# GpSimd products for a third of the key chunks, and TensorE transposes of q and k, in a hybrid attention block

## The chip, the cores and the metric

The kernel runs on one core of a Trainium2 chip. The metric is device time in microseconds (us) of one execution. The core has five engines that run their own instruction streams in order and meet at semaphores: TensorE (PE; its weight loads are listed apart as PEld), VectorE (DVE), ScalarE (ACT), GpSimd (POOL) and SyncE (SP), which here only issues DMAs. Lines such as L563 are lines of the kernel before; in the changed kernel everything behind the edits stands 12 to 14 lines further down.

## The reference

One layer of a residual trunk, 2048 tokens of width 1024 in float32: RMSNorm, one combined projection, four heads of differential attention and eight heads of stick-breaking attention, an output projection, RMSNorm and a SwiGLU feed-forward block (2816 wide). The change lies in the stick-breaking part:

```python
def one_block(args):
    qb, blk = args
    q_pos = blk * QBLK + jnp.arange(QBLK, dtype=jnp.int32)
    z = jnp.einsum('bqhd,bkhd->bhqk', qb, k).astype(jnp.float32) * scale
    mask = (k_pos[None, :] < q_pos[:, None])[None, None]
    log_1mb = jnp.where(mask, jax.nn.log_sigmoid(-z), 0.0)
    rem = lax.cumsum(log_1mb, axis=3, reverse=True) - log_1mb
    a = jnp.where(mask, jnp.exp(jax.nn.log_sigmoid(z) + rem), 0.0)
    return jnp.einsum('bhqk,bkhd->bqhd', a.astype(v.dtype), v)
```

With beta = sigmoid(z), the weight of key s for query t is beta(t,s) times the product of 1 - beta over the keys between s and t.

## The kernel before

Matrix products are made in fp16 with both operands split into a high and a low half, three products for one. The heads are worked in eight groups g: 0 to 3 hold one differential head each, 4 to 7 two stick-breaking heads each. While group g is in attention, a stream (`proj_stream`) projects group g+1: 16 token tiles of 24 matmuls (L325) into one of two PSUM banks tagged "pj", read out as v and as q and k by `proj_out` (casts L332 or L334, residuals L335). After every fourth tile `proj_batch` transposes q and k: two DMA transposes of 8 blocks of 128x128 from the tile st into qT[:, 2:4] and kT (L377), and two DMA copies that exchange the upper and lower 64 partitions of q into qT[:, 0:2] (L379). So the score matmuls have a q with high and low half swapped. All of these DMAs stand in SP's one queue.

A stick-breaking group runs 48 units (`stage_a`): a query tile i of 128 rows, a head m and a block b of up to 1024 keys. A unit takes two tiles of a ring of nine ("z4", 128x1028 float32), om and be. Per chunk of up to 512 keys, from the last to the first: scores in a PSUM bank sc (L453, four banks); ACT writes sigmoid(-z) into om (L559) and sigmoid(z) = beta back into the score bank (L560); DVE scans om backwards to running products (L562; the score bank is its second operand, which the operation bypasses); DVE multiplies beta and the shifted om into be (L563). Then `split_t` casts be to fp16 on ACT (L89, tile s of a ring of three), subtracts for the low half on GpSimd (L98), and a DMA transposes both halves into aT (L408). Five units later `stage_b` multiplies aT with v on PE (L463).

A helper chooses engines when the program is built: `pick` adds an operation's cost to a ledger for each engine and takes the one with the lowest sum, and `level` clears the ledgers at every fourth query tile. `note` books work that has no choice. Casts (`to16`: L89 ACT, L91 DVE, L93 GpSimd), `tt` and `split_psum` are chosen so. The order of each engine's instructions is then made by a scheduler that simulates the program; it is fixed before the run.

The output projection of finished token tiles (L766) starts beside the last group, and the FFN follows from about 1465 us on.

Of the kernel before, what the change touches and what calls it, by code (L numbers as in the profile page):

```python
# [11 lines left out]
F32 = mybir.dt.float32  # L12
F16 = mybir.dt.float16
BF16 = mybir.dt.bfloat16
I32 = mybir.dt.int32
AF = mybir.ActivationFunctionType
ALU = mybir.AluOpType
# [4 lines left out]
S, D, P = 2048, 1024, 128  # L22
# [37 lines left out]
def block(tc, a, out):  # L60
    nc = tc.nc
    PE, ACT, DVE, POOL, SP = nc.tensor, nc.scalar, nc.vector, nc.gpsimd, nc.sync
    top = ExitStack()
    with top:
# [8 lines left out]
        def note(e, ns):  # L73
            load[e] += ns * KW[e]

        def pick(**cost):
            e = min(cost, key=lambda k: load[k] + cost[k] * KW[k])
            load[e] += cost[e] * KW[e]
            return e

        def level():
            for k in load:
                load[k] = 0.0

        def to16(dst, src, n, engines="ADP", psum=False):
            cost = {"A": 0.84 * n + 110, "D": (1.05 if psum else 0.53) * n + 70, "P": 1.1 * n + 80}
            e = pick(**{k: cost[k] for k in engines})
            if e == "A":
                ACT.copy(dst, src)  # L89
            elif e == "D":  # L90
                DVE.tensor_copy(dst, src)  # L91
            else:
                POOL.tensor_scalar(dst, src, 1.0, 0.0, op0=ALU.mult, op1=ALU.add)  # L93

        def tt(dst, a_, b_, op, n, engines="DP"):
            cost = {"D": 1.15 * n + 70, "P": 2.45 * n + 80}
            e = pick(**{k: cost[k] for k in engines})
            (DVE if e == "D" else POOL).tensor_tensor(dst, a_, b_, op)  # L98

        def pri(k):  # L100
            def deco(f):
                @functools.wraps(f)
                def g(*args):
                    with tc.high_priority(PRI[k]) if PRI[k] else nullcontext():
                        return f(*args)
                return g
            return deco

        def nm(s):
            uid[0] += 1  # L110
            return f"{s}{uid[0]}"
# [7 lines left out]
        id16 = cp.tile([P, P], F16, name="id16")  # L119
# [25 lines left out]
        def rstd(dst, ss, mul, eps):  # L145
            n = dst.shape[-1]
            if n > 1:
                ACT.activation(dst, ss, AF.Identity, bias=eps, scale=mul)
            else:
                DVE.tensor_scalar(dst, ss, mul, eps, op0=ALU.mult, op1=ALU.add)  # L150
            POOL.tensor_tensor(dst, dst, mhalf[:, :n], ALU.pow)
# [100 lines left out]
        psj = top.enter_context(tc.tile_pool(name="psj", bufs=2, space=PSUM, side="right"))  # L252
# [3 lines left out]
        with ExitStack() as ph1:  # L256
# [6 lines left out]
            def z4():  # L263
                return zp.tile([P, 1028], F32, tag="z4", bufs=ZB, name=nm("z4"))
# [87 lines left out]
            @pri("pb")  # L352
            def proj_batch(g, G, B):
                st, v, raw = B
                qT = sp.tile([P, 4, 4, P], F16, tag="qT", bufs=QB, name=nm("qT"))
                kT = sp.tile([P, 2, 4, P], F16, tag="kT", bufs=KB, name=nm("kT"))
                if g < 4:
                    rq = raw[:].rearrange("p t (c e) -> p t c e", e=64)
                    sq = st[:].rearrange("p c t s e -> p (c t s e)")[:, :2048].bitcast(F32)
                    ACT.activation(sq.rearrange("p (t c e) -> p t c e", t=4, c=4), rq, AF.Square)  # L360
                    note("A", 950)
                    ss = sm.tile([P, 16], F32, tag="ss", bufs=2, name=nm("ss"))
                    DVE.tensor_reduce(ss[:], sq.rearrange("p (c e) -> p c e", e=64), op=ALU.add, axis=AX.X)
                    rs = sm.tile([P, 16], F32, tag="rs", bufs=2, name=nm("rs"))
                    rstd(rs[:], ss[:], 2.0 ** -16 / 64, G["epsk"][:])
                    rsb = rs[:].rearrange("p (t c) -> p t c", c=4).unsqueeze(3).to_broadcast([P, 4, 4, 64])
                    DVE.tensor_tensor(rq, rq, rsb, ALU.mult)
                    note("D", 2300)
                    gb = gk[:].unsqueeze(1).unsqueeze(1).to_broadcast([P, 4, 2, 64])
                    tt(rq[:, :, 2:4, :], rq[:, :, 2:4, :], gb, ALU.mult, 512)  # L370
                    for o in range(2):
                        src = rq[:, :, 2 * o : 2 * o + 2, :]
                        d = st[:, 2 * o : 2 * o + 2].rearrange("p c t s e -> p t c s e")
                        to16(d[:, :, :, 0, :], src, 512)
                        tt(d[:, :, :, 1, :], src, d[:, :, :, 0, :], ALU.subtract, 512)
                for T, c in ((qT[:, 2:4], 0), (kT[:], 2)):
                    SP.dma_start_transpose(T.rearrange("p c t n -> p (c t) n"), st[:, c : c + 2].rearrange("p c t s e -> p (c t s e)"))  # L377
                for o in (0, 64):
                    SP.dma_start(qT[o : o + 64, 0:2].rearrange("p c t n -> p (c t n)"), qT[64 - o : 128 - o, 2:4].rearrange("p c t n -> p (c t n)"))  # L379
                G["q"].append(qT)  # L380
                G["k"].append(kT)
                G["v"].append(v)
# [63 lines left out]
            def fq(g, i):  # L446
                k = 2 if g == NG - 1 else 4
                return (i % k, k)
# [92 lines left out]
            def sb_attn(g, G):  # L541
                last = {}

                @pri("at")
                def stage_a(i, m, b):
                    L = (i + 1) * 128
                    n = min(1024, L - 1024 * b)
                    be, om = z4(), z4()
                    if b == i // 8:
                        DVE.memset(om[:, n : n + 1], 8192.0)  # L550
                    else:
                        DVE.tensor_copy(om[:, n : n + 1], last[m][:, 0:1])
                    last[m] = om
                    for c in range((n - 1) // 512, -1, -1):
                        lo, hi = 512 * c, min(512 * c + 512, n)
                        w = hi - lo
                        sc = ps.tile([P, 512], F32, tag="sc", bufs=4, name=nm("sc"))
                        score_chunk(G, sc, i, 2 * b + c, m, w // P, b == i // 8 and hi == n)
                        ACT.activation(om[:, lo:hi], sc[:, :w], AF.Sigmoid, scale=G["nkz"][:])  # L559
                        ACT.activation(sc[:, :w], sc[:, :w], AF.Sigmoid, scale=G["kz"][:])  # L560
                        ov = om[:, lo:hi][:, ::-1]
                        DVE.tensor_tensor_scan(ov, ov, sc[:, :w], om[:, hi : hi + 1], op0=ALU.mult, op1=ALU.bypass)  # L562
                        DVE.tensor_tensor(be[:, lo:hi], sc[:, :w], om[:, lo + 1 : hi + 1], ALU.mult)  # L563
                        note("A", 1.7 * w + 400)
                        note("D", 3.15 * w + 350)
                    return n, split_t(be[:, :n], n, "A", "P")

                ypd = {}

                def stage_b(i, m, b, n, aT):  # L570
                    r, k = fq(g, i)
                    if i // k not in ypd:
                        ypd[i // k] = ps.tile([P, 512], F32, tag="yp", name=nm("yp"))
                    yp = ypd[i // k]
                    pv(G, yp, P * r + 64 * m, aT, b, n, 128 * m, 64, r == 0 and m == 0 and b == i // 8, r == k - 1 and m == 1 and b == 0)
                    if m == 1 and b == 0 and r == k - 1:
                        finish(g, G, i, k, yp)
                        G["fin"] = i + 1

                pend = []  # L580
                done = 0
                for i in range(NT):
                    if i % 4 == 0:
                        level()
                    for b in range(i // 8, -1, -1):
                        for m in range(2):
                            n, aT = stage_a(i, m, b)
                            pend.append((i, m, b, n, aT))
                            if len(pend) > PD:
                                stage_b(*pend.pop(0))  # L590
                            done += n // P + CS
                            yield done / (272 + 48 * CS), (i + 1 if b == 0 and m == 1 else i)
                for u in pend:
                    stage_b(*u)
# [640 lines left out]
```

## Time and profile before

| | us |
|---|---|
| median of 3 runs (2754.74 to 2759.51) | 2757.65 |
| profiled execution | 2755.86 |
| its span, first to last instruction | 2754.1 |
| first and last stick-breaking scan (L562) starts | 612.6 and 1395.6 |
| last projection weight load (L325) starts | 1203.4 |
| first FFN weight load (L943) starts | 1465.0 |

The profile gives each engine's busy time and the span in 40 slices of 68.9 us with busy tenths. A row of a group of instructions has line, engine, operation, output and inputs, shapes and count; then busy us and the mean ns of one; then the engine's idle time just before them and what ended it. A row of waits has who waited for whom, us in total, times, longest us. Granted clock is the TensorE clock that the throttle granted, 1 being full speed.

### The profile page before, as it was taken

Reading aid. Unit: us, or ns where it says so; the run is one execution under the profiler, and the core shown is the slowest. Engines: PE = TensorE matmul, PEld = TensorE weight load, DVE = VectorE, ACT = ScalarE, POOL = GpSimd, SP = SyncE. Lnnn points to the kernel's source line nnn. Section 1 sums busy time; section 2 is a strip of 40 time slices with the busy share of each in tenths; the row PEclk is TensorE's granted clock in tenths of the full one; section 3 lists DMA queues with packets and bytes.
Section 4 is the critical chain, followed back from the end, with each engine's and each line's share of the span. In section 5 each row is a group of like instructions: output and inputs, shape, how many; then the busy total and the mean of one; then the engine's idle time right before and its main releaser. Section 6 shows DMA issues by size and latency. Waiting matters only on the chain. (4 is left out here: it accounts for less than half of the span.)

```text
span 2754.1 us, 45485 instructions
## 1 busy us (share of the span) xinstructions
PE 2491.4 (90%) x17084; PEld 1411.9 (51%) x17084; DVE 1997.4 (73%) x3782; ACT 1361.3 (49%) x2543; POOL 1447.6 (53%) x1008
## 2 busy tenths in 40 slices
PE   7998989888888786888989899999999999999998
PEld 4665555555555453457775444444444444444443
DVE  6898879787889989986655877777785544444445
ACT  4665656566878778765644535444352212111121
POOL 2578767655455545546565656565574232322323
PEclk9999999999999987999999999999999999999999
DMA  6788787789999988987797675656658834635534
GB/s 225 201 170 184 148 189 163 173 172 203 196 217 191 198 175 156 199 196 208 199 272 273 218 241 199 220 196 226 235 182 307 315 146 164 229 136 198 207 121 167
DMA packets 649133, 551.91 MB, mean 200 GB/s; under 512 B 506624, under 2 KB 574208, under 8 KB 638672
## 3 DMA queue, kind: packets, MB, share of 16 engines
q1 hardware_dynamic: 647088, 546.92, 72.0%
q8 instruction: 134, 2.20, 0.3%
q0 software_dynamic: 512, 1.36, 0.2%
q10 hardware_dynamic: 1312, 0.72, 0.1%
q14 instruction: 87, 0.71, 0.1%
HBM read 265.27 MB, written 151.52 MB: 151 GB/s over the span
## 5 line engine op out<-in xcount | busy, mean ns | idle before, releaser
L98 POOL TENSOR_TENSOR s<-z,s 128x1024 f16<-128x1024 f32 (+7 forms) x288 | 473.9, 1653 | 334.1 <-ACT s L89 291.2
L325 PE MATMUL pj<-w,xt 128*128 128x384 f16 x3072 | 572.2, 334 | 29.3 <-DVE st L335 12.1
L325 PEld LDWEIGHTS <-xt 128*128 128x128 f16 x3072 | 300.2, 100 | 239.9 <-issue 37.3
L453 PE MATMUL sc<-kT,qT 128*128 128x512 f16 (+3 forms) x1280 | 348.7, 363 | 72.0 <-DVE z L563 33.0
L1041 PE MATMUL pd<-wd,act 128*128 128x512 f16 x1848 | 406.0, 379 | 3.4 <-DVE hs L1047 2.4
L562 DVE TENSOR_TENSOR_SCAN z<-z,sc 128x512 f32<-128x512 f32 (+3 forms) x320 | 355.5, 1113 | 69.4 <-ACT sc L560 67.5
L463 PE MATMUL yp<-v,aT 128*128 128x64 f16 (+1 forms) x4896 | 282.0, 208 | 76.4 <-DMA aT<-s 75.7
L463 PEld LDWEIGHTS <-aT 128*128 128x128 f16 x4896 | 246.5, 102 | 165.1 <-DMA aT<-s 101.7
L943 PEld LDWEIGHTS <-wg 128*128 128x128 f16 x1848 | 182.3, 99 | 247.3 <-issue 37.3
L1041 PEld LDWEIGHTS <-act 128*128 128x128 f16 x1848 | 180.7, 98 | 222.3 <-issue 4.6
L943 PEld LDWEIGHTS <-wu 128*128 128x128 f16 x1848 | 181.8, 98 | 219.7 <-issue 7.2
L98 POOL TENSOR_TENSOR hs<-hs,cu 128x512 f32<-128x512 f32 x132 | 166.8, 1268 | 239.8 <-DVE cu L1047 86.3
L98 POOL TENSOR_TENSOR act<-cg,act 128x512 f16<-128x512 f32 x117 | 166.6, 1437 | 231.4 <-ACT act L999 125.1
L98 POOL TENSOR_TENSOR fst<-fst 128x512 f32<-128x512 f32 x97 | 182.5, 1882 | 157.3 <-DVE wd L220 85.9
L1047 DVE SCALAR_TENSOR_TENSOR hs<-pd,c,hs 128x512 f32<-128x512 f32 x192 | 142.3, 749 | 163.0 <-PE pd L1041 161.5
L89 ACT CAST s<-z 128x384 f16<-128x384 f32 (+7 forms) x216 | 170.2, 789 | 151.5 <-DMA aT<-s 61.9
L559 ACT ACTIVATE z<-sc,c 128x512 f32<-128x512 f32 (+3 forms) x320 | 203.3, 635 | 10.2 <-PE sc L453 6.7
L563 DVE TENSOR_TENSOR z<-sc,z 128x512 f32<-128x512 f32 (+3 forms) x320 | 193.4, 606 | 8.1
L560 ACT ACTIVATE sc<-sc,c 128x512 f32<-128x512 f32 (+3 forms) x320 | 195.6, 611 | 0.0
L999 ACT CAST act<-cg 128x512 f16<-128x512 f32 x132 | 81.3, 616 | 222.1 <-DVE cg L1005 175.8
L766 PE MATMUL po<-wo,mt 128*128 128x256 f16 x1536 | 182.0, 277 | 6.9 <-DVE xf L769 4.9
L943 PE MATMUL pm<-X,wg 128*128 128x512 f16 x792 | 179.1, 379 | 0.2 <-ACT bx L1116 0.2
(233 smaller groups left out, 4026.5 us busy)
## 6 DMA issues: line engine op xcount, KB each, us to landing
xt<-xs SPq DMA_DIRECT2D x112, 512.0 KB, 4.4
hs<-hd SPq DMA_DIRECT2D x96, 512.0 KB, 4.3
hd<-hs SPq DMA_DIRECT2D x80, 512.0 KB, 3.5
split<-wg SPq DMA_DIRECT2D x11, 1792.0 KB, 11.4
split<-wu SPq DMA_DIRECT2D x11, 1792.0 KB, 10.3
split<-wd SPq DMA_DIRECT2D x11, 1792.0 KB, 10.5
wg<-split SPq DMA_DIRECT2D x11, 1792.0 KB, 7.2
wd<-split SPq DMA_DIRECT2D x11, 1792.0 KB, 8.2
```

Of the source, the lines that this page charges most:

```text
L89: ACT.copy(dst, src)
L98: (DVE if e == "D" else POOL).tensor_tensor(dst, a_, b_, op)
L325: PE.matmul(pj[:, :384], lhsT=xv[:, xi, kt, :], rhs=G["w"][:, wi, kt, :], start=n == 0, stop=n == 23)
L453: PE.matmul(sc[:, : 128 * w].rearrange("p (t n) -> p t n", n=P), lhsT=G["q"][i // 4][:, 2 - 2 * o + m, i % 4, :], rhs=G["k"][q][:, m, 0:w, ...
L463: PE.matmul(yp[:, y0 : y0 + wd], lhsT=aT[:, a_, :], rhs=v[:, v_ : v_ + wd], start=start and j == 0 and q == 0, stop=stop and j == nb - 1 a ...
L559: ACT.activation(om[:, lo:hi], sc[:, :w], AF.Sigmoid, scale=G["nkz"][:])
L560: ACT.activation(sc[:, :w], sc[:, :w], AF.Sigmoid, scale=G["kz"][:])
L562: DVE.tensor_tensor_scan(ov, ov, sc[:, :w], om[:, hi : hi + 1], op0=ALU.mult, op1=ALU.bypass)
L563: DVE.tensor_tensor(be[:, lo:hi], sc[:, :w], om[:, lo + 1 : hi + 1], ALU.mult)
L766: PE.matmul(po[:, sl], lhsT=mt[:, kt, P * xi : P * xi + P], rhs=wos[2 * h + n][wi][:, kt, :], start=q == 0, stop=q == 23)
L943: PE.matmul(ps_[:].rearrange("p (t n) -> p t n", n=P), lhsT=wv[:, wo, wi, 128 * kt : 128 * kt + 128], rhs=X[xo][:, :, xi, kt, :], start=st ...
L1041: PE.matmul(po[:], lhsT=act[:, ao, xi, 128 * j : 128 * j + 128], rhs=W["d"][:, wo, wi, :], start=start and u == 0 and q == 0, stop=u == nu ...
```

## The change

In `stage_a` each chunk's product may go to GpSimd. `pick` compares DVE at 1.04 w + 155 ns and GpSimd at 2.4 w + 100 ns for w keys. If GpSimd is taken, ACT writes beta to be in SBUF and not to the score bank, and GpSimd multiplies be by om in place; the scan then has the raw scores as its bypassed operand.

In `proj_batch`, for groups 5 to 7, PE transposes q and k into a "pj" bank, seen as 1024 fp16 columns: one bank for kT, one for qT[:, 2:4], one for the swapped qT[:, 0:2], whose blocks are made in two halves of 64 rows. ACT or DVE copies each bank out. The DMA transposes and copies stay for groups 0 to 4.

```diff
-                for T, c in ((qT[:, 2:4], 0), (kT[:], 2)):
-                    SP.dma_start_transpose(T.rearrange("p c t n -> p (c t) n"), st[:, c : c + 2].rearrange("p c t s e -> p (c t s e)"))
-                for o in (0, 64):
-                    SP.dma_start(qT[o : o + 64, 0:2].rearrange("p c t n -> p (c t n)"), qT[64 - o : 128 - o, 2:4].rearrange("p c t n -> p (c t n)"))
+                if g > 4:
+                    for T, c, sw in ((kT[:], 2, 0), (qT[:, 2:4], 0, 0), (qT[:, 0:2], 0, 1)):
+                        pt = psj.tile([P, 512], F32, tag="pj", name=nm("qkt"))[:].bitcast(F16)
+                        for b in range(8):
+                            blk = st[:, c + b // 4, b % 4]
+                            if sw:
+                                for o in range(2):
+                                    PE.transpose(pt[64 * o : 64 * o + 64, P * b : P * b + P], blk[:, 1 - o, :], id16[:])
+                            else:
+                                PE.transpose(pt[:, P * b : P * b + P], blk.rearrange("p s e -> p (s e)"), id16[:])
+                        to16(T.rearrange("p c t n -> p (c t n)"), pt, 1024, "AD", True)
+                else:
+                    ...
                         ACT.activation(om[:, lo:hi], sc[:, :w], AF.Sigmoid, scale=G["nkz"][:])
-                        ACT.activation(sc[:, :w], sc[:, :w], AF.Sigmoid, scale=G["kz"][:])
+                        e = pick(D=1.04 * w + 155, P=2.4 * w + 100)
+                        beta = sc[:, :w] if e == "D" else be[:, lo:hi]
+                        ACT.activation(beta, sc[:, :w], AF.Sigmoid, scale=G["kz"][:])
                         ov = om[:, lo:hi][:, ::-1]
                         DVE.tensor_tensor_scan(ov, ov, sc[:, :w], om[:, hi : hi + 1], op0=ALU.mult, op1=ALU.bypass)
-                        DVE.tensor_tensor(be[:, lo:hi], sc[:, :w], om[:, lo + 1 : hi + 1], ALU.mult)
+                        (DVE if e == "D" else POOL).tensor_tensor(be[:, lo:hi], beta, om[:, lo + 1 : hi + 1], ALU.mult)
                         note("A", 1.7 * w + 400)
-                        note("D", 3.15 * w + 350)
+                        note("D", 2.08 * w + 200)
```

The order of the built programs shows where the instructions stand. On GpSimd, in group 4 (be is z_9302, z_9342, z_9367 and so on, one a unit; s is the fp16 pair), before:

```order
L98 TENSOR_TENSOR s_9313<-z_9302,s_9313 128x512
L98 TENSOR_TENSOR s_9353<-z_9342,s_9353 128x512
L98 TENSOR_TENSOR s_9384<-z_9367,s_9384 128x1024
L98 TENSOR_TENSOR s_9415<-z_9398,s_9415 128x1024
L98 TENSOR_TENSOR s_9495<-z_9477,s_9495 128x640
```

and in the changed kernel, at the same units:

```order
L98 TENSOR_TENSOR s_9313<-z_9302,s_9313 128x512
L577 TENSOR_TENSOR z_9367<-z_9367,z_9368 128x512 x2
L98 TENSOR_TENSOR s_9353<-z_9342,s_9353 128x512
L577 TENSOR_TENSOR z_9477<-z_9477,z_9478 128x512
L98 TENSOR_TENSOR s_9384<-z_9367,s_9384 128x1024
L98 TENSOR_TENSOR s_9415<-z_9398,s_9415 128x1024
L98 TENSOR_TENSOR s_9495<-z_9477,s_9495 128x640
```

Products (L577) of newer units now stand between the residuals of older ones. On DVE, at the unit of z_9367 and z_9368, before (a scan is printed as a SCALAR_TENSOR_TENSOR of L562):

```order
L562 SCALAR_TENSOR_TENSOR z_9368<-z_9368,sc_9370 128x512
L563 TENSOR_TENSOR z_9367<-sc_9370,z_9368 128x512
L552 COPY z_9399<-z_9343 128x1
L562 SCALAR_TENSOR_TENSOR z_9368<-z_9368,sc_9377 128x512
L335 SCALAR_TENSOR_TENSOR st_10013<-pj_10132,st_10013 128x4x64
L563 TENSOR_TENSOR z_9367<-sc_9377,z_9368 128x512
L562 SCALAR_TENSOR_TENSOR z_9399<-z_9399,sc_9401 128x512
```

and now:

```order
L576 SCALAR_TENSOR_TENSOR z_9368<-z_9368,sc_9370 128x512
L91 COPY kT_9872<-qkt_9873 128x1024
L576 SCALAR_TENSOR_TENSOR z_9368<-z_9368,sc_9377 128x512
L576 SCALAR_TENSOR_TENSOR z_9399<-z_9399,sc_9401 128x512
L91 COPY qT_9871<-qkt_9893 128x1024
L577 TENSOR_TENSOR z_9398<-sc_9401,z_9399 128x512
```

Both products of this unit are gone from DVE, and two copies of transposed q and k stand between the scans. On SP, in the same group, before (qT and kT are the transposed q and k, aT the transposed weights, xt an input tile of the projection):

```order
L408 DMA_TRANSPOSE aT_9545<-s_9542 128x10x128
L377 DMA_TRANSPOSE qT_10403<-st_10013 128x8x128
L377 DMA_TRANSPOSE kT_10404<-st_10013 128x8x128
L408 DMA_TRANSPOSE aT_9610<-s_9607 128x16x128
L379 DMA qT_10403<-qT_10403 64x1024
L408 DMA_TRANSPOSE aT_9644<-s_9641 128x16x128
L379 DMA qT_10403<-qT_10403 64x1024
```

and now:

```order
L420 DMA_TRANSPOSE aT_9545<-s_9542 128x10x128
L420 DMA_TRANSPOSE aT_9610<-s_9607 128x16x128
L403 DMA xt_10884<-xs 128x2048
L420 DMA_TRANSPOSE aT_9644<-s_9641 128x16x128
```

The four DMAs of the batch have left SP's queue. On PE, before, this stretch has no matmul on st; now, inside a projection tile (qkt is the bank of the transposes, id the identity):

```order
L325 MATMUL pj_10408<-w_8277,xt_10406 128x384
L385 LDWEIGHTS st_10047
L385 MATMUL qkt_10439<-id_68,st_10047 128x128
L385 LDWEIGHTS st_10047
L385 MATMUL qkt_10439<-id_68,st_10047 128x128
L385 LDWEIGHTS st_10047
L385 MATMUL qkt_10439<-id_68,st_10047 128x128
L325 LDWEIGHTS xt_10406
```

Three transposes of a batch stand between matmuls of one projection tile; the others follow in runs of up to 16, with attention work between the runs.

More of the change, by code (lines that the diff above doesn't have):

```diff
@@ L375, in proj_batch @@
                         tt(d[:, :, :, 1, :], src, d[:, :, :, 0, :], ALU.subtract, 512)
-                for T, c in ((qT[:, 2:4], 0), (kT[:], 2)):
-                    SP.dma_start_transpose(T.rearrange("p c t n -> p (c t) n"), st[:, c : c + 2].rearrange("p c t s e -> p (c t s e)"))
-                for o in (0, 64):
-                    SP.dma_start(qT[o : o + 64, 0:2].rearrange("p c t n -> p (c t n)"), qT[64 - o : 128 - o, 2:4].rearrange("p c t n -> p (c t n)"))
+                if g > 4:
[10 more added lines that the diff above has]
+                else:
+                    for T, c in ((qT[:, 2:4], 0), (kT[:], 2)):
+                        SP.dma_start_transpose(T.rearrange("p c t n -> p (c t) n"), st[:, c : c + 2].rearrange("p c t s e -> p (c t s e)"))
+                    for o in (0, 64):
+                        SP.dma_start(qT[o : o + 64, 0:2].rearrange("p c t n -> p (c t n)"), qT[64 - o : 128 - o, 2:4].rearrange("p c t n -> p (c t n)"))
                 G["q"].append(qT)
```

## The prediction

> **What bounds the kernel now.** First the page's shares, for the whole program.
>
> ```profile
> PE 2491.4 (90%) x17084; PEld 1411.9 (51%) x17084; DVE 1997.4 (73%) x3782; ACT 1361.3 (49%) x2543; POOL 1447.6 (53%) x1008
> PE   7998989888888786888989899999999999999998
> DVE  6898879787889989986655877777785544444445
> ```
>
> PE looks like the bound, but the share is a mean over stages: in slices 9 to 17 (about 610 to 1200 us) DVE shows 9 where PE shows 8 or less. That is stick-breaking attention, the only place that the change touches. So next the busy time by stretch (columns: us, then PE, PEld, DVE, ACT, POOL busy with counts, granted clock, DMA share, GB/s).
>
> ```profile
> 612.00:1200.00 588.00, 473.07 (x4803) 295.59 (x4801) 519.51 (x933) 457.75 (x880) 304.46 (x196) 0.92 0.95 192
> 1200.00:1400.00 200.00, 176.13 (x1826) 145.15 (x1825) 144.86 (x235) 123.42 (x212) 115.22 (x79) 0.96 0.78 198
> 1700.00:2754.00 1054.00, 1021.83 (x4741) 465.82 (x4739) 607.13 (x831) 281.01 (x379) 447.68 (x315) 0.99 0.56 203
> ```
>
> From 612 to 1200 DVE is busy 519.5 of 588 us (88%), PE 80%, ACT 78%, GpSimd 52%, and the DMA engines 95%. From 1200 to 1400 the output projection fills PE (88%) and DVE has room; the FFN is PE's (97%). So what the change can win lies in the 588 us, which hold all the projections of the last three groups. Then who waits for whom there:
>
> ```profile
> POOL s L98 <- ACT s L89: 230.2, 110, 5.7
> PE yp L463 <- DMA aT<-s: 38.2, 34, 3.5
> PE sc L453 <- DVE z L563: 31.3, 33, 1.8
> PE sc L453 <- DVE z L550: 12.5, 16, 1.7
> PE sc L453 <- DVE z L552: 8.7, 9, 1.8
> PE pj L325 <- DVE st L335: 9.5, 9, 2.3
> ACT s L89 <- DMA aT<-s: 35.7, 32, 4.4
> DVE z L562 <- ACT sc L560: 33.7, 43, 2.1
> ```
>
> PE waits 52.5 us (31.3 + 12.5 + 8.7) for score banks that DVE has not read yet, and 38 us for transposed weights; DVE's idle time is half (33.7 of 68.5) waiting for the second sigmoid. GpSimd's waits cost nothing by themselves. DVE is the tightest, with DMA latency and PE close behind.
>
> **The products.** Rows by shape, 612 to 1400 us, which hold all 320 chunks:
>
> ```profile
> L562 DVE TENSOR_TENSOR_SCAN z<-z,sc 128x512 f32<-128x512 f32 x224 | 285.0, 1273 | 41.7 <-ACT sc L560 40.8 <-PE sc L455 0.4
> L563 DVE TENSOR_TENSOR z<-sc,z 128x512 f32<-128x512 f32 x224 | 153.4, 686 | 5.6
> L563 DVE TENSOR_TENSOR z<-sc,z 128x384 f32<-128x384 f32 x32 | 17.7, 553 | 0.9
> L563 DVE TENSOR_TENSOR z<-sc,z 128x256 f32<-128x256 f32 x32 | 13.4, 419 | 0.7
> L563 DVE TENSOR_TENSOR z<-sc,z 128x128 f32<-128x128 f32 x32 | 9.2, 288 | 0.8
> L98 POOL TENSOR_TENSOR z<-z,z 128x512 f32<-128x512 f32 x7 | 9.0, 1282 | 5.0 <-DVE z L98 4.6
> L98 POOL TENSOR_TENSOR s<-z,s 128x1024 f16<-128x1024 f32 x83 | 182.5, 2202 | 161.4 <-ACT s L89 147.6 <-issue 9.0 <-DMA aT<-s 3.0
> L559 ACT ACTIVATE z<-sc,c 128x512 f32<-128x512 f32 x224 | 157.0, 701 | 5.9 <-PE sc L453 4.4 <-PE sc L455 1.4
> L560 ACT ACTIVATE sc<-sc,c 128x512 f32<-128x512 f32 x224 | 151.8, 678 | 0.0
> ```
>
> The built order has 155 of the 320 products on GpSimd, nearer a half than a third: 122 of 512 columns, 7 of 384, 17 of 256, 9 of 128. DVE loses 122 x 0.686 + 7 x 0.553 + 17 x 0.419 + 9 x 0.288 = 97 us. GpSimd gets 122 x 1.282 = 156 us, and 21 us for the smaller ones at the same 2.5 ns a column: 177 us. By groups the 155 split 36, 37, 37, 45, and the 588 us hold 264 of the 320 chunks, so some 123 of 155 fall there (79%): DVE -77, GpSimd +140. ACT writes beta to SBUF: 701 against 678 ns, 123 x 0.023 = 3 us. For a GpSimd chunk the scan no longer reads beta, so it need not wait for the second sigmoid, and the score bank comes free after the scan, one 0.686 us product earlier. Both cut at the 33.7 and 31.3 us above; I book nothing for them apart.
>
> **What the planner sends the other way.** With DVE's ledger lower, 45 v and 21 q/k casts go from ACT to DVE, and the 36 new evictions split 15 to DVE, 21 to ACT.
>
> ```profile
> L332 ACT ACTIVATE st<-pj 128x256 f16<-128x256 f32 x57 | 22.6, 396 | 17.1 <-DVE v L335 16.6 <-DVE m L195 0.5
> L335 DVE SCALAR_TENSOR_TENSOR st<-pj,st 128x256 f16<-128x256 f32 x57 | 23.0, 404 | 3.5 <-ACT st L332 3.4
> L332 ACT ACTIVATE v<-pj 128x128 f16<-128x128 f32 x56 | 16.5, 297 | 10.9 <-PE pj L325 10.1 <-PE yp L463 0.5
> L335 DVE SCALAR_TENSOR_TENSOR v<-pj,v 128x128 f16<-128x128 f32 x57 | 15.7, 276 | 11.6 <-ACT v L332 11.6
> L89 ACT CAST s<-z 128x1024 f16<-128x1024 f32 x80 | 83.9, 1050 | 70.1 <-DVE z L563 18.7 <-issue 16.1 <-DMA xcd<-x 13.8
> L98 DVE TENSOR_TENSOR x<-z,x 128x1024 f16<-128x1024 f32 x4 | 5.3, 1328 | 0.0
> ```
>
> DVE: 45 x 0.276 + 21 x 0.404 = 21 us. A DVE eviction of 1024 columns is not in the trace: between the 0.686 of one 512-column row and two of them, 1.37; I take 1.2, so 18 us (10 to 21). Together +39, net on DVE -77 + 39 = -38. ACT: -45 x 0.297 - 21 x 0.396 + 21 x 1.05 = 0. After 1200 us 18 element-wise operations of the output stage also move from GpSimd to DVE, at most 18 x 1.33 = 24 us if each were as long as the last row. DVE is at 72% there and PE at 88%, which hides them; uncovered they would cost that.
>
> **The transposes.** PE gets 384 (12 batches of 8 + 8 + 16 halves).
>
> ```profile
> L766 PE MATMUL po<-wo,mt 128*128 128x256 f16 x1040 | 124.6, 277 | 4.9 <-DVE xf L769 4.9
> L455 PE MATMUL sc<-tri,idb 128*128 128x128 bf16 x124 | 28.9, 234 | 0.0
> L377 SPq DMA_TRANSPOSE qT<-st x15: 1232/1255/2679, 624.9 to 1212.0; - x15
> ```
>
> In a run, 256 columns take 124.6/1040 = 0.12 us, so 128 take 0.06; alone, one takes 0.234. So 384 cost 23 to 90 us; the order has them in runs of 3 to 16, so I take 23, all of it on PE between 612 and 1200. Their three tiles share the two pj banks with the projections: 9 of 56 tiles waited 9.5 us in all for a bank, 0.17 a tile; 36 more are 6 us, to be expected in PE's idle share, not on top. Off SP go 24 transposes, such as the 1.26 us row, and 24 copies behind them, and the DMA engines lose 192 blocks of 128x128 (12 x 16) beside the 2176 of the attention weights (8 heads x 2 x 136), 8%. That eases the 38 and 36 us of aT waits; the bound is nothing to 8% of 588, and I book nothing for it apart.
>
> The Trainium skill, "VectorE: DVE Perf Modes", The three transpose paths, gives 390 ns for a 128x128 transpose on TensorE. By it the 384 would cost an estimated 150 us, not 23; the run row speaks against it.
>
> **The sum.** DVE goes to 519.5 - 38 = 481, PE to 473 + 23 = 496, ACT 461, GpSimd 304 + 140 = 444. PE is now the most loaded. If DVE still set the pace at its 88%, the stretch would shrink to 481/0.883 = 545, by 43 us. If PE does at the 88% that it reaches in the next stretch, where this attention still runs beside it, it is 496/0.88 = 564, by 24. I take the second: four engines within 15% of each other wait for one another. The rest stays: orders before the first stick-breaking tile and in nearly all of the FFN are the same. The profiled execution took 2755.9 (span 2754.1), 1.8 under the median 2757.65, within its runs' spread: 2755.9 - 24 = **2732**.
>
> **Rivals.**
> - *DVE sets the pace to the end.* The earlier scan starts and the eased DMA let PE keep up: -43, **2713**. For it: 52.5 us of PE's 115 us idle are DVE's. Against: PE would have to be 91% busy. 17%.
> - *The transposes eat it.* If they run in short pieces at some 0.12 us (46 us, between both rows), PE has 519, at 88% 590 us: +2, **2758**. For it: three tiles on two banks. Against: the runs in the order. 11%.
> - *Slower: the ring of nine z4 tiles.* Each unit takes two, so a sigmoid of unit n writes where unit n-4's residual has been read: the way from first sigmoid to residual must fit four units, 4 x 588/160 = 14.7 us. Bare it is now 2 x (0.70 + 0.68) + 1.27 + 0.69 + 1.05 + 2.20 = 8.0; with a product on GpSimd 8.6, and 12.1 behind one residual and one product of others in GpSimd's queue, which is in order. Behind two of each it is 15.6, and each of the 83 wide units costs (15.6 - 14.7)/4 = 0.22: +18, **2774**, the relief lost. It decides from 14.7 us on. For it: GpSimd at 76% and a ring no larger. Against: GpSimd waits 230 us today, and the order places uses later (the value product follows its scores by 6.0 units on average, before 4.7). 16%.
> - *The port.* A two-SBUF-input DVE operation could wait for a product on GpSimd.
>
> ```profile
> L220 DVE SCALAR_TENSOR_TENSOR w<-wst,sW,w 128x1536 f16<-128x1536 f32 x6 | 12.8, 2125 | 0.4 <-POOL w L219 0.4
> ```
>
> The 6 such weight rows, with 8 for the output weights and 10 norm rows, make 24; at GpSimd's added share, 24%, each blocked by 1.28 us: 24 x 0.24 x 1.28 = 7 us, **2739**. The scans have the score bank in PSUM as one input. 6%. The Trainium skill, "SBUF — State Buffer", Who interferes with whom, says that a DVE instruction with two SBUF inputs contends with a GpSimd one that reads SBUF, and the second to issue blocks. The trace neither bears it out nor refutes it: the residual beside scans takes 2.20 us for 1024 columns.
>
> That the change doesn't do what it says is no rival: the order shows the products and transposes.
>
> **How the numbers follow.** Forecast 50%, 2732, its own range 2720 to 2745. With the rivals: faster 0.50 + 0.17 + 0.06 = 0.73, same 0.11, slower 0.16. About 0.2% (5.5 us) is what a measurement here can tell from no change. The range, 8 in 10, runs from 2706, a little below the fast rival (DMA's relief on top), to 2768, which leaves out most of the slow one.
>
> **What would show it.** Right: DVE's busy time up to the same group boundary 35 to 45 us lower, GpSimd's 140 higher, PE's share there at 87 to 89%, its waits for score banks well under 52 us. The scans behind GpSimd chunks no longer wait for the second sigmoid. Wrong: ACT sigmoids waiting for GpSimd residuals (the ring), PE waiting for qkt evictions, transposes near 0.23 us, or products over 1.3 us beside scans.

## The result, and the profile after

| | us |
|---|---|
| kernel before, median of 15 runs (2751.43 to 2762.62) | 2755.25 |
| changed kernel, median of 15 runs (2736.61 to 2754.31) | 2747.43 |
| ratio, 95% interval | 0.9963 [0.9951, 0.9975] |
| profiled execution of the changed kernel (span 2752.5) | 2754.31 |

The kernel is faster by 0.37%, some 10 us (2755.25 x 0.0037; 7 to 14 by the interval; the medians alone differ by 7.8). The forecast was 24; the median lies in the stated range of 2706 to 2768 and above the forecast's own, 2720 to 2745. The profiled execution is the longest of the fifteen, 1.6 us under the profiled one of the kernel before, so what a change is worth is taken from the ratios below, and the profiles show only where the time goes. One execution of all those below, of the transposes alone at planner cost 1.3, took 9014 us where its five others took 2773 to 2781, and is left out of its ratio.

First the stretches that carried the prediction, in the changed kernel (columns as before: us, then PE, PEld, DVE, ACT, POOL busy with counts, granted clock, DMA share, GB/s).

```profile
612.00:1200.00 588.00, 489.70 (x5252) 315.89 (x5249) 495.04 (x911) 468.61 (x859) 431.65 (x328) 0.94 0.89 181
1200.00:1400.00 200.00, 173.47 (x1835) 145.74 (x1836) 136.77 (x200) 118.58 (x197) 125.75 (x86) 0.95 0.72 185
1700.00:2754.00 1054.00, 1023.05 (x4738) 466.00 (x4735) 603.41 (x828) 279.45 (x378) 445.90 (x313) 0.99 0.56 203
```

GpSimd takes 432 us where it took 304, DVE 495 where it took 520, though more is done: this stretch holds 273 scans now and held 264. The next three rows are the scans, in the same stretch (columns: us, DVE busy with its count, granted clock, DMA share, GB/s), before and after, each in its own fence.

```profile
612.00:1200.00 588.00, 290.67 (x264) 0.92 0.95 192
```

```profile
612.00:1200.00 588.00, 297.10 (x273) 0.94 0.89 181
```

Since the two stretches hold different amounts of work, the next two rows end where the 264th scan starts, at 1186.4 us before and at 1175.8 after (all columns, before and after, each in its own fence).

```profile
612.00:1186.40 574.40, 460.70 (x4685) 287.70 (x4683) 515.11 (x924) 454.75 (x873) 300.62 (x194) 0.92 0.95 191
```

```profile
612.00:1175.80 563.80, 467.03 (x5018) 301.13 (x5016) 477.21 (x871) 453.91 (x831) 416.94 (x315) 0.94 0.89 180
```

Up to the same scan DVE is busy 38 us less (515.11 - 477.21), GpSimd 116 us more and PE 6 us more, and the scan starts 10.6 us earlier. PE, however, is at 83% (467.03/563.8), not at the 88% of the forecast. Who waits for whom from 612 to 1200 us, after:

```profile
POOL s L98 <- ACT s L89: 69.3, 48, 6.3
POOL z L577 <- DVE z L576: 68.4, 44, 5.2
ACT s L89 <- DMA aT<-s: 62.5, 38, 6.1
PE yp L475 <- DMA aT<-s: 36.4, 40, 2.4
DVE z L576 <- ACT sc L574: 33.0, 31, 4.9
DVE z L576 <- ACT z L574: 25.6, 27, 2.5
PE sc L465 <- DVE z L576: 21.1, 26, 5.0
PE sc L465 <- DVE z L562: 12.0, 17, 1.4
PE sc L465 <- DVE z L577: 9.7, 9, 3.2
PE sc L465 <- DVE z L564: 7.5, 6, 2.2
```

PE still waits 50.3 us for score banks (21.1 + 12.0 + 9.7 + 7.5; 52.5 before). DVE itself now waits 58.6 us for sigmoids (33.0 + 25.6; 33.7 before), and ACT 62.5 us for aT transposes to free the ring of three s tiles (35.7 before). GpSimd waits 69 us for casts where it waited 230, and 68 us for scans; it is still idle for 156 of the 588 us. In this stretch DVE is busy 24 us less and waits 25 us more for sigmoids: what it was relieved of came back as waiting.

The wait that the change should have ended is still there. In a GpSimd chunk the scan (L576) doesn't read what the second sigmoid (L574) writes, yet in the timeline (columns: start us, duration us, engine, line, operation; in brackets the idle time before and what ended it) it starts behind it:

```profile
900.73 0.68 ACT L571 ACTIVATE z<-sc,c 128x512 f32<-128x512 f32 x1
901.31 0.68 ACT L574 ACTIVATE z<-sc,c 128x512 f32<-128x512 f32 x1
902.02 1.28 DVE L576 TENSOR_TENSOR_SCAN z<-z,sc 128x512 f32<-128x512 f32 x1 [1.82 <-ACT z L574]
```

The first sigmoid, all that the scan needs, ends at 901.41; the second at 901.99, and the scan starts 0.03 us later. So it is wherever a scan waited for a sigmoid there: the groups of waits above name a second sigmoid (L574) in all 58 and the first (L571) in none. In 31 of the 58 the scan belongs to a DVE chunk and reads the bank that L574 writes (sc); in the other 27 (z) it does not. Over the whole trace, none of the 155 scans of GpSimd chunks starts before its chunk's second sigmoid has ended.

### The profile page after: what moved, and what is told of

It reads as the page before. It is cut to its first block, busy times and chain, and to the rows that moved or that the text cites. A ratio compares the mean times of both kernels' runs of the same rounds, so it can differ in the third digit from the quotient of the medians.

```text
span 2752.5 us, 46252 instructions
## 1 busy us (share of the span) xinstructions
PE 2499.2 (91%) x17468; PEld 1426.0 (52%) x17468; DVE 1964.6 (71%) x3726; ACT 1364.3 (50%) x2501; POOL 1574.3 (57%) x1142
## 5 line engine op out<-in xcount | busy, mean ns | idle before, releaser
L576 DVE TENSOR_TENSOR_SCAN z<-z,sc 128x512 f32<-128x512 f32 (+3 forms) x320 | 353.1, 1112 | 78.9 <-ACT z L574 37.5
L465 PE MATMUL sc<-kT,qT 128*128 128x512 f16 (+3 forms) x1280 | 343.2, 358 | 65.9 <-DVE z L576 21.1
L577 POOL TENSOR_TENSOR z<-z,z 128x512 f32<-128x512 f32 (+2 forms) x155 | 161.6, 1047 | 105.8 <-DVE z L576 87.2
L571 ACT ACTIVATE z<-sc,c 128x512 f32<-128x512 f32 (+3 forms) x320 | 208.4, 654 | 21.7 <-PE sc L467 8.8
L957 PE MATMUL pm<-X,wu 128*128 128x512 f16 x792 | 179.1, 379 | 0.0
## 6 DMA issues: line engine op xcount, KB each, us to landing
split<-wu SPq DMA_DIRECT2D x11, 1792.0 KB, 10.1
```

Of the source, the lines that this page charges most:

```text
L465: PE.matmul(sc[:, : 128 * w].rearrange("p (t n) -> p t n", n=P), lhsT=G["q"][i // 4][:, 2 - 2 * o + m, i % 4, :], rhs=G["k"][q][:, m, 0:w, ...
L577: (DVE if e == "D" else POOL).tensor_tensor(be[:, lo:hi], beta, om[:, lo + 1 : hi + 1], ALU.mult)
L957: PE.matmul(ps_[:].rearrange("p (t n) -> p t n", n=P), lhsT=wv[:, wo, wi, 128 * kt : 128 * kt + 128], rhs=X[xo][:, :, xi, kt, :], start=st ...
```

## The experiments

All ratios are to the kernel before, run in turn on the same chip. The first eight ran on one chip, the eight on the order on two others, the last two on a fourth, so between these groups only ratios are compared.

**The two halves apart.** One kernel has only the transposes (`pick` is offered DVE alone), one only the products.

```diff
# transposes only
-                        e = pick(D=1.04 * w + 155, P=2.4 * w + 100)
+                        e = pick(D=1.04 * w + 155)
# products only
-                if g > 4:
+                if g > NG:
```

> Only PE's transposes; all products stay on DVE (pick has DVE alone). Ring theory (the products on GpSimd delay the residuals, and ACT, whose casts wait for a free tile of the ring of three s tiles, loses the gain): this part alone is worth the DMA relief and costs 23 us of PE and 35 evictions on ACT, so within 4 us of before (ratio 0.9985 to 1.0015), with ACT's waits for aT at or under the 36 us of before. PE theory (the transposes and their two banks eat the gain): slower than before by 8 us or more, ratio above 1.003.

> Only the products on GpSimd; q and k of all groups are transposed by DMA as before. Ring theory: the same gain as the whole change or less, ratio 0.996 to 1.000, with ACT's waits for aT at 60 us or more from 612 to 1200 us, since DMA has its 8% back. PE theory: more gain than the whole change, ratio under 0.993, since PE's 23 us are gone.

Measured: transposes alone 1.0054 [1.0042, 1.0067], products alone **0.9930 [0.9919, 0.9942]**. The products are the gain, the transposes a loss; the products alone beat both kernels. Both came out as the PE theory had it, the second at the edge of its range, and outside the ranges of the ring theory. The sum of the two, -0.16%, is less than the -0.37% of both together.

**The ring of three s tiles.** On ACT the wait that grew most is that for aT transposes. A fourth s tile (paid for with one of two y tiles) takes it away.

```diff
-QB, KB, ZB, AB, SB, PD = 4, 7, 9, 5, 3, 5
+QB, KB, ZB, AB, SB, PD = 4, 7, 9, 5, 4, 5
-                y = sp.tile([P, 512], F32, tag="y", bufs=2, name=nm("y"))
+                y = sp.tile([P, 512], F32, tag="y", bufs=1, name=nm("y"))
```

> The whole change with four s tiles in place of three (one y tile in place of two pays for the space). Ring theory: ACT's waits for aT from 612 to 1200 us fall from 62 to under 35 us, DVE's waits for the sigmoids with them, and the time to 2725 to 2736 us, ratio 0.989 to 0.993 to before. PE theory: the waits fall, the time does not, ratio 0.995 to 0.998.

> Control: the kernel before with the same four s tiles and one y tile. Ring theory: the ring was no bound there, as 36 us of ACT's waits stood beside 12% of idle time that DVE did not lose to it; ratio 0.997 to 1.001. If the ring was a bound already, under 0.996, and the gain of the fourth tile belongs to no part of the change.

> Products on GpSimd alone, q and k by DMA, four s tiles. If the ring of three holds back the products: ratio 0.988 to 0.991, 5 to 12 us faster than products alone with three. If DMA does, whose engines are busy 99% there with products alone: as fast as with three, 0.992 to 0.994.

Measured: changed kernel with four 0.9940 [0.9925, 0.9954], kernel before with four 0.9981 [0.9970, 0.9992], products with four 0.9984 [0.9975, 0.9993]. In the first of them the waits fell as far as one could wish:

```profile
DVE z L576 <- ACT sc L574: 31.9, 27, 3.5
DVE z L576 <- ACT z L574: 14.6, 21, 2.8
ACT s L89 <- DMA aT<-s: 12.1, 11, 2.1
PE sc L465 <- DVE z L577: 6.3, 7, 1.8
PE sc L465 <- DVE z L576: 6.1, 13, 1.0
PE sc L465 <- DVE z L562: 4.0, 6, 1.4
PE sc L465 <- DVE z L564: 3.7, 4, 1.1
```

ACT's wait for aT is 12 us instead of 62, PE's for score banks 20 instead of 50, and the time moved by about 0.2%, as it did in the kernel before. The ring theory's 0.989 to 0.993 did not come. With products alone a fourth tile cost 0.5%, outside both ranges named for it, and why is open. The ring is not where the gain went.

**Doses of the transposes, in the changed kernel.** Each transpose issued twice; each eviction made twice; all evictions on DVE.

```diff
# twice on TensorE
-                                for o in range(2):
+                                for o in (0, 1, 0, 1):
-                                PE.transpose(pt[:, P * b : P * b + P], blk.rearrange("p s e -> p (s e)"), id16[:])
+                                for _ in range(2):
+                                    PE.transpose(pt[:, P * b : P * b + P], blk.rearrange("p s e -> p (s e)"), id16[:])
# evictions twice: this line once more; all on DVE: "D" for "AD"
                         to16(T.rearrange("p c t n -> p (c t n)"), pt, 1024, "AD", True)
```

> The whole change with every transpose of q and k issued twice on PE (384 more matmuls, 53 to 60 ns each in a run, 20 to 23 us of PE work; evictions as in the change). PE-work theory (what the transposes cost is their time on PE): 15 to 23 us slower than the whole change, ratio to before 1.002 to 1.005. Eviction theory (the cost lies in the copies out of the banks, on ACT and DVE): within 5 us of the whole change, ratio 0.994 to 0.998.

> The whole change with every bank of transposed q and k copied out twice (36 more copies of 0.68 us on DVE or 1.03 us on ACT, 24 to 37 us of work there; PE as in the change, each bank held longer). Eviction theory: 8 to 18 us slower than the whole change, ratio 0.999 to 1.003. PE-work theory: within 5 us of the whole change, ratio 0.994 to 0.998.

> The whole change with all 36 copies on DVE, where one takes 0.69 us, not 1.03 as on ACT (21 copies move; the planner moves other casts back to ACT). Eviction theory, with ACT as the one that holds up DVE: 3 to 10 us faster than the whole change, ratio 0.992 to 0.996. PE-work theory: no difference, 0.995 to 0.998.

Measured: 0.9983 [0.9974, 0.9993], 0.9968 [0.9957, 0.9979] and 0.9963 [0.9950, 0.9975], beside 0.9963 of the changed kernel. A second set of transposes costs 0.2%, about 5 us, less than the 15 to 23 of the PE-work theory; a second set of evictions costs nothing that can be told, and moving them nothing, so the eviction theory fails in this kernel. With the second set of transposes the granted clock from 612 to 1200 us was 0.96 and not 0.94; part of their work may be hidden by that, and the runs don't separate the two.

**The order.** The scheduler that makes the instruction order is moved by any edit. So all four kernels were built with two other planner costs for a score group, 1.3 and 0.8 in place of 1.0. No instruction of the kernel before is added or taken away by this.

```diff
-LAG0, LAG, PF, CD, CS, LO = 0, 8, 8, 1.0, 1.0, 0.5
+LAG0, LAG, PF, CD, CS, LO = 0, 8, 8, 1.0, 1.3, 0.5
```

> The kernel before with CS = 1.3 for 1.0, which shifts by a little where projection tiles are recorded among the units; same instructions, another order. Content theory (the times of the parts come from their work): 0.999 to 1.001 to before. Order theory (an order that the scheduler makes differs by as much as the parts): outside 0.998 to 1.002.

> Transposes on PE alone in that other order. Content theory: slower than before again, 1.004 to 1.007. Order theory: the 15 us of the first order do not come back, 0.998 to 1.003.

> Products on GpSimd alone in that other order. Content theory: 0.991 to 0.995 again. Order theory: outside, most likely between 0.995 and 1.000, as the first order was the best of four kernels with products.

> The whole change in that other order. Content theory: 0.995 to 0.998 again. Order theory: outside.

> The kernel before with a planner cost of 0.8 us for a score group in place of 1.0: no instruction added or removed, only the order changes. If the order is worth as much as the change (as with 1.3, where it gave 0.9971), this differs from before by 0.2 to 0.5% in either direction; if the order is of no account, 0.999 to 1.001.

> Transposes on TensorE alone in the third order. If they cost work of TensorE that nothing hides (20 to 26 us of busy time more in two orders), this is 0.5 to 1.1% slower than e13. If their cost was a matter of order, it is within 0.3% of e13 or faster.

> Products on GpSimd alone in the third order. If they are a gain by work, 0.2 to 0.8% faster than e13, with 2.10 to 2.15 us per key chunk up to the last projection against 2.2 in e13. If the 0.7% in the first order was mostly order, within 0.2% of e13 or slower.

> The changed kernel in the third order. If both signs belong to the work and their sizes are about the means of the two orders so far (products 0.4% gained, transposes 0.8% lost), this would be 0 to 0.4% slower than e13; by the finding that both together gain (0.4% in the first order, 0.14% in the second), 0.1 to 0.4% faster than e13.

| planner cost | before | transposes | products | both |
|---|---|---|---|---|
| 1.0 | 1 | 1.0054 [1.0042, 1.0067] | 0.9930 [0.9919, 0.9942] | 0.9963 [0.9951, 0.9975] |
| 0.8 | 1.0001 [0.9990, 1.0012] | 1.0059 [1.0044, 1.0074] | 0.9945 [0.9932, 0.9957] | 0.9957 [0.9944, 0.9969] |
| 1.3 | 0.9971 [0.9959, 0.9983] | 1.0077 [1.0058, 1.0095] | 0.9956 [0.9938, 0.9973] | 0.9957 [0.9941, 0.9973] |

Within each row, transposes lose 0.5 to 1.1%, products gain 0.15 to 0.7%, and both together gain 0.14 to 0.44%. The signs are the same in all three; in the last row the intervals of the products (0.9938 to 0.9973) and of both overlap that of the kernel before, so there the two gains aren't clear of noise. The sizes don't hold: an order by itself moved the kernel before by 0.3%, nearly as much as the whole change. And the halves are not independent. Beside products that stay on DVE the transposes cost 0.54, 0.58 and 1.06%; beside products on GpSimd 0.33, 0.12 and 0.01%.

**What the transposes cost where they cost most.** In the kernel with transposes alone the planner sets 35 of 36 evictions on ACT, which also has 191 of the 192 casts of v and of q and k; with the products, DVE's ledger is lower, and DVE takes 67 of the casts and 15 evictions. The choice is by these costs (n is the number of columns):

```python
cost = {"A": 0.84 * n + 110, "D": (1.05 if psum else 0.53) * n + 70, "P": 1.1 * n + 80}
```

So two edits of the kernel with transposes alone: all evictions on DVE (the casts stay where they are), and every transpose twice, both written as above.

> Transposes alone with all 36 evictions on VectorE (0.69 us each, 25 us) in place of ScalarE (1.03 us each, 36 us). If ScalarE's evictions are the cost (sigmoids late, scans late), most of the 0.54% goes: 0.999 to 1.002 beside before. If VectorE sets the pace there, 25 us more of it make it worse: 1.008 to 1.012. If the cost is TensorE's work, 1.004 to 1.007 as with transposes alone.

> Transposes alone, each issued twice, the second to the same place: some 20 us more TensorE work, evictions as they were. If TensorE's work is what costs where the products stay on VectorE, another 15 to 25 us: 1.011 to 1.015 beside before. If it is the evictions or the waits, 1.005 to 1.008.

Measured: 1.0014 [1.0006, 1.0023] and 1.0057 [1.0044, 1.0070], beside 1.0054. Doubling TensorE's transposes adds nothing that can be told; moving the evictions gives 0.40% back. The scans' waits with evictions on ACT (transposes alone), then with evictions on DVE:

```profile
DVE z L576 <- ACT sc L574: 44.5, 51, 2.3
```

```profile
DVE z L576 <- ACT sc L574: 22.7, 28, 2.2
```

and the stretch from 612 to 1200 us, in the same sequence, with the doubled transposes as a third:

```profile
612.00:1200.00 588.00, 474.98 (x4947) 299.88 (x4944) 512.20 (x909) 475.35 (x894) 295.11 (x192) 0.90 0.85 171
```

```profile
612.00:1200.00 588.00, 479.72 (x5109) 309.40 (x5107) 542.54 (x970) 457.18 (x886) 302.37 (x196) 0.94 0.88 177
```

```profile
612.00:1200.00 588.00, 484.20 (x5376) 316.19 (x5375) 518.10 (x925) 480.43 (x903) 302.44 (x195) 0.93 0.85 174
```

Two groups of evictions by shape, on ACT with transposes alone and on DVE in the edit (busy us, mean ns of one, idle before):

```profile
L89 ACT COPY qT<-qkt 128x1024 f16<-128x1024 f16 x23 | 24.8, 1079 | 1.3 <-PE qkt L383 1.3
```

```profile
L91 DVE COPY qT<-qkt 128x1024 f16<-128x1024 f16 x24 | 16.2, 673 | 0.2 <-PE qkt L385 0.2
```

DVE, the busiest engine, was given more work and the kernel became faster: it went from 512 to 543 us, 92% of the stretch, and waits 23 us for sigmoids and not 45. This is what one would see if an eviction on ACT, which takes 1.08 us there and stands ahead of sigmoids in ACT's queue, made DVE wait behind it; on DVE it takes 0.67. The planner booked 1.05 x 1024 + 70 ns = 1.15 us for it on DVE and 0.84 x 1024 + 110 = 0.97 on ACT: its table makes DVE dearer, the trace cheaper. The account is supported, not shown. The 0.40% is larger than any change of order alone moved the kernel before (0.29%), though not by much, and the edit was tried in one order. The granted clock in the stretch also differs, 0.90 with evictions on ACT and 0.94 with them on DVE, and no run holds it still. With the transposes doubled it was 0.93 (third row); there the projections' matmuls took 182 ns of PE's busy time each (228.4 us for 1257), with single transposes 188 (236.4 for 1259). So the nothing that doubling adds may be work offset by a faster clock. Of the two edits, timed on one chip at about the same clock, the one with evictions on DVE is the faster by 0.4%, but it also lacks the second transposes.

## Why the prediction was right or wrong

**DVE's relief: right.** Net -38 us was forecast, and up to the same scan it was -38. Two prices were too dear: GpSimd gained 116 us there, not 140, since a product of 512 columns took 1.16 us in the mean and 1.09 in the median, not 1.28; and an eviction on DVE took 0.69 us, not 1.2, so that 15 of them are 10 us, not 18.

Of the changed kernel, the instructions of the product's line (min/median/max in ns, first and last start), and then of the tile qkt:

```profile
L577 POOL TENSOR_TENSOR z<-z,z x155: 402/1092/2618, 629.5 to 1391.7; 128x512 f32<-128x512 f32 x122, 128x256 f32<-128x256 f32 x17, 128x128 f32<-128x128 f32 x9, 128x384 f32<-128x384 f32 x7
```

```profile
L91 DVE COPY qT<-qkt x12: 662/691/692, 727.3 to 1209.9; 128x1024 f16<-128x1024 f16 x12
L91 DVE COPY kT<-qkt x3: 664/667/692, 723.8 to 1051.8; 128x1024 f16<-128x1024 f16 x3
L385 PE MATMUL qkt<-id,st x192: 217/219/314, 719.1 to 1209.6; 128*128 128x128 f16 x192
```

**The transposes' size: right.** The next row is the stretch for the tile qkt alone in the changed kernel (us, then PE, DVE and ACT busy, granted clock, DMA share, GB/s).

```profile
612.00:1200.00 588.00, 24.94 (x355) 9.55 (x14) 19.70 (x19) 0.94 0.89 181
```

355 of the 384 take 24.9 us of PE, 0.07 each; 23 us for all was forecast. PE's load up to the same scan rose by only 6 us (460.7 to 467.0), though, where 23 were added in the sum: its other matmuls took less time there, at a granted clock of 0.94 and not 0.92. How much of that is the clock is open. The Trainium skill's 390 ns ("VectorE: DVE Perf Modes", The three transpose paths) would have made an estimated 138 us of these 355. The rows above show 0.219 us for a single one, and in a run they overlap; the measurement decides against the figure.

**"PE is at 88% there": the step that failed.** It turned -38 us of DVE and +23 of PE into -24 us by letting PE rise to the share that it reaches in the next stretch. It reached 83%, up from 80. No row of before showed that PE can reach 88% in this stretch: the next one has the output projection to fill PE, and here the waits for score banks, which were to fall well under 52 us, are 50. The load that the forecast gave PE erred the other way: by its own division the 467 us that PE was really busy would have taken 531 at 88%, and they took 564 at 83%. Three things stood in the way, and the forecast had none of them as a term; what each is worth isn't measured.
- *The scan still waits for the second sigmoid.* "It need not wait" was true of the data, not of the program. 25.6 of DVE's 58.6 us of waits are such, in 27 places. Since the second sigmoid begins about 0.6 us behind the first, up to an estimated 27 x 0.6 = 16 us of DVE's waits hang on it. Both touch the score bank: the second sigmoid reads the scores there, and the scan takes them as its bypassed operand. That the program keeps the two apart on that bank would explain all 155 scans, but it isn't tested; no kernel was run whose scan has its bypassed operand elsewhere.
- *The transposes cost more than PE's time, probably through ACT.* The forecast priced ACT at "0" by its busy time. With the evictions on ACT and no casts taken off it, the transposes cost 0.54%; with evictions on DVE, 0.14%. If what counts is what stands ahead of a sigmoid in ACT's queue, the changed kernel is spared most of it because the planner, seeing DVE lighter, moved casts away; this would be how the halves help each other, and why all evictions on DVE bring nothing there (0.9963 both). It is argued from the runs and not shown: the transposes alone with casts moved off ACT weren't tried.
- *Part of the gain is handed back after 1200 us, in two orders of three.* In the profiled executions at planner cost 1.0 the last projection matmul, the chunks done by then, the FFN's first weight load and the time between are (times in us):

| | last projection | chunks by then | FFN starts | between |
|---|---|---|---|---|
| before | 1203.5 | 266 | 1465.0 | 261.5 |
| transposes alone | 1234.9 | 275 | 1487.7 | 252.8 |
| products alone | 1184.2 | 269 | 1452.3 | 268.1 |
| changed | 1196.7 | 273 | 1466.3 | 269.6 |

Products alone finish the projections 19 us earlier and start the FFN 13 earlier; the changed kernel 7 earlier and, in this longest of its runs, not at all. At planner cost 1.3 the changed kernel's lead over the kernel before in the same order falls likewise, from 10.0 us (1200.4 and 1190.4) to 1.5 (1451.7 and 1450.2); at 0.8 it doesn't, 7.1 (1205.5 and 1198.4) and 10.1 (1463.2 and 1453.1). So this belongs to the order as much as to the change. Rows of the changed kernel and of before at planner cost 1.0, from the last projection to within half a us of the FFN's first weight load, show what fills the rest:

```profile
1196.70:1465.80 269.10, 232.13 (x2414) 196.94 (x2413) 174.11 (x264) 142.51 (x225) 156.77 (x107) 0.96 0.79 226
```

```profile
1203.50:1465.00 261.50, 234.93 (x2382) 198.01 (x2380) 177.89 (x286) 143.52 (x232) 153.69 (x102) 0.96 0.83 233
```

PE has 232 and 235 us of work left there in both, the output projection above all, and the little that was won in front appears as more idle PE behind (37 us for 27).

**The rivals.** *DVE sets the pace* is refuted as it was put: DVE's share fell to 84% while PE waited for score banks as long as before, and with the evictions on DVE, DVE reached 92% in a kernel faster than the one beside it. *The transposes eat it*: some of it, 0.0 to 0.33% of 0.15 to 0.70%, but not by short pieces on PE, since they took 0.07 us each and not 0.12; doubling them costs 0.2% beside the products and nothing that can be told without. *The ring of nine z4 tiles* didn't show: first sigmoids waited 1.6 us in all for a residual.

```profile
ACT z L571 <- POOL s L98: 1.6, 1, 1.6
```

*The port*: the rows that it named did get longer, by 8 x 0.50 + 6 x 0.52 = 7.1 us, as much as it was priced at (below, the row of before that the prediction doesn't show, then the changed kernel, then transposes alone). That is no sign of the products: with transposes alone, and no product on GpSimd, they took 1786 and 2841 ns, 8 x 0.24 + 6 x 0.72 = 6.2 us more than before, and with products alone 1780 and 2048, 1.4 us more. What lengthened them is open. The scans, one of whose inputs is in PSUM, kept their length (1272 ns after, 1273 before). This agrees with the Trainium skill ("SBUF — State Buffer", Who interferes with whom), whose rule is on two SBUF inputs, without proving it.

```profile
L220 DVE SCALAR_TENSOR_TENSOR wo<-z,sW,wo 128x1024 f16<-128x1024 f32 x8 | 12.4, 1551 | 0.0
```

```profile
L220 DVE SCALAR_TENSOR_TENSOR wo<-z,sW,wo 128x1024 f16<-128x1024 f32 x8 | 16.4, 2053 | 0.0
L220 DVE SCALAR_TENSOR_TENSOR w<-wst,sW,w 128x1536 f16<-128x1536 f32 x6 | 15.9, 2648 | 0.0
L576 DVE TENSOR_TENSOR_SCAN z<-z,sc 128x512 f32<-128x512 f32 x224 | 283.2, 1272 | 41.7 <-ACT z L574 21.6 <-ACT sc L574 17.3
```

```profile
L220 DVE SCALAR_TENSOR_TENSOR w<-wst,sW,w 128x1536 f16<-128x1536 f32 x6 | 17.0, 2841 | 0.1
L220 DVE SCALAR_TENSOR_TENSOR wo<-z,sW,wo 128x1024 f16<-128x1024 f32 x8 | 14.2, 1786 | 0.0
```

**The DMA's relief: no sign of it.** The DMA share fell from 0.95 to 0.89, and PE's waits for aT went from 38.2 to 36.4 us, ACT's from 35.7 to 62.5; with transposes alone they are 39.4 and 31.9, at a share of 0.85. Products alone keep every DMA transpose, at a share of 0.99, and are the fastest kernel of all. That nothing was booked for it was right.

**What stays open.** How much the products gain by themselves is known only to 0.15 to 0.7%, because the order weighs as much. That a scan released at the first sigmoid would return the 16 us was not tried. And the granted clock moved with the changes, from 0.90 to 0.96 in the stretch: no run tells how much of each ratio is the clock, and whether a better fed PE was granted more or ran better because it was.

## What to carry to other kernels

Work taken off the busiest engine counts only if that engine was not about to wait for the next one: before booking the gain, ask what it waits for today, and what stands ahead of that in the other engine's queue. Price a small operation by where it stands in an in-order queue, and not only by the load of its engine: in the one order tried, the transposes cost 15 us (0.54%) with their 35 copies of 1 us on ScalarE, and 4 (0.14%) with them on VectorE, the busier of the two. Where a scheduler makes the order, time both halves of a change apart and in more than one order before believing a third of a per cent.

## What the runs showed of the hardware

- A copy of 128x1024 fp16 from PSUM took 0.67 to 0.69 us on DVE, as long as a 128x512 float32 product with one PSUM input (0.686), and 1.01 to 1.08 us on ACT (medians and means of groups).
- A 128x512 float32 product from SBUF to SBUF on GpSimd took 1.09 us in the median and 1.16 in the mean, 1.6 to 1.7 times the 0.686 of DVE's product with one input in PSUM; the 1.28 us of seven operations of this shape before was too dear.
- In the changed kernel's executions a higher granted clock mostly went with a shorter time: 2754 us at 0.969, 2749 to 2752 at 0.971 and 0.972, 2744 to 2748 at 0.973 and 0.974, and 2739 and 2741 at 0.976; one of the fifteen stands apart, 2737 at 0.974. It isn't so in every kernel here: products alone at planner cost 1.3 took 2739 us at 0.965 and 2745 at 0.969. The fifteen span 18 us, so a difference of 10 between two profiled executions says little by itself.
